# Weights and values in block order in DRAM, casts tied to TensorE, stores moved from ScalarE to SP

## The chip, the cores and the metric

The kernel runs on one core of a Trainium2 chip. A core has TensorE (PE; its weight loads are PEld), VectorE (DVE), ScalarE (ACT), GpSimd (POOL) and SyncE (SP), which only issues transfers, and 16 DMA engines that SP's and ScalarE's transfers share. The metric is device time in microseconds of one execution, as the median of several runs.

## The reference

Two layers of a hybrid backbone over 1024 latent and 256 context tokens of width 1024, in float32:

```
p = (layer_norm(x) * (1 + scale) + shift) @ w_in      # 7072 columns; ctx the same, with its own modulation
ya = neighbourhood attention(p[0:768])     # 4 heads of 64, 8x16 window, relative bias, plus the context
yb = latent attention(p[768:1184])         # low-rank q and kv, 4 heads, rotary key part
yc = bidirectional RG-LRU(p[1184:1440])    # conv of width 4, one linear scan per direction
yd = grouped-query attention(p[1440:1952]) # 4 heads, 2 kv heads, RMS norm, rotary
z, m = p[1952:2976], p[2976:7072]          # per branch: 256 columns of z, 1024 of m
out = sum_i sigmoid(m_i) * ((y_i * silu(z_i)) @ w_branch[i]) @ w_out
x = layer_norm(alpha * x + gate * out) * ln_g + ln_b
```

Every attention reads all context keys as well. Layer 1 needs the latent rows only.

## The kernel before, in words

All products are made of float32r pieces: each operand is split into a high part (a cast on ScalarE) and a low part (a subtraction on VectorE), and three matmuls replace one (`mm_a`, `mm_b`, lines 292 to 307). The modulated input stays in SBUF as `xh`, `xl`. Weights come through `load_w` (266): a DMA from SP into one of two `wraw` tiles, then `split_w` (248) casts (line 259) into `whi` and subtracts (260) into `wlo`. `load_chunk` (283) fetches a block of 1024 x 128 as two such loads of 512 rows, so a run in DRAM is 128 columns of a row of `w_in`, 512 B.

A layer runs through these stages, and the labels in front of tile names tell in which of them an instruction was written down:

- `g_proj`, `m_proj`, `a_proj` and `lru` project the tokens. `put_t` stores queries and keys transposed to DRAM, `put_v` (355) the values, token by token, by transfers from ScalarE.
- `g_att`, `m_att`, `a_att` are the attentions of branches D, B and A, four heads each. A head works through units of two or three query tiles of 128 (a unit of context queries first, in layer 0). `fetch` (907) loads the queries one unit ahead, `ahead_kv` (917) the next head's keys and values at a head's second unit (`i == 1`). The scores go to `wide` (line 660; 874 and 876 in branch A), VectorE takes the maximum (662), ScalarE the exponential (636, 640), TensorE transposes the probabilities (605), ScalarE and VectorE split them (310, 311) and TensorE multiplies them with the values (612, 613). The half sums are joined through a `tmp` tile (627). `load_q` (667) and `load_k` (678) read a source whose outermost dimension is two: 64 rows twice, or high and low part.
- Beside that, two fillings keep TensorE busy. `gates()` (941) computes 16 of the layer's 32 blocks of m (those in `gate_d`), in steps that `tick` hands out; each result is copied to a `tmp` tile (954) and stored from ScalarE (955). `put_u` (436), queued after every second head, computes a block of z, applies it to the head pair's output and stores that from ScalarE (466). It loads its weight block as it begins (438). `put_u` also ends each half of the LRU.
- `merge` loads the stored gates, or computes the other 16 blocks of m, multiplies with `w_branch` and sums; `outp` applies `w_out` and the layer norm.

There are three `tmp` tiles, two `wraw` tiles and, from the attention on, six pairs of `whi` and `wlo`, three blocks' worth.

The order in which an engine works is fixed before the run. The program is written down once, and a planner then puts each instruction onto its engine's queue as soon as, by its own estimate of durations, its inputs are there and a buffer is free; among those ready the one written down first goes first. An instruction can thereby move far ahead of its place in the program. On the chip each engine follows its queue in order and waits at semaphores.

Of the kernel before, what the change touches and what calls it, by code (L numbers as in the profile page):

```python
# [8 lines left out]
F32 = mybir.dt.float32  # L9
# [7 lines left out]
D = 1024  # L17
# [20 lines left out]
W_B = 26  # L38
UNITS = [(2, 3), (5, 3), (8, 2)]
# [7 lines left out]
def hybrid_kernel(ctx: ExitStack, tc, a):  # L47
# [200 lines left out]
    def split_w(raw, shape, far=False):  # L248

        n = 1  # L250
        for d in shape[1:]:
            n *= d
        if far:
            both = slot(F32R, w=1024, s="wboth")
            hi, lo = both[:, :512], both[:, 512:]
        else:
            hi = cut["wp"].tile([128, 512], F32R, tag="whi", name=nm("whi"))
            lo = cut["wp"].tile([128, 512], F32R, tag="wlo", name=nm("wlo"))
        act.copy(hi[:, :n], raw[:, :n])  # L259
# [6 lines left out]
    def load_w(src, shape, far=False):  # L266
# [8 lines left out]
        return split_w(raw, shape, far)  # L275
# [4 lines left out]
    def load_rows2(w2, c0):  # L280
        return [load_w(w2[k * 128:(k + 1) * 128, c0:c0 + 512], [128, 512]) for k in range(2)]

    def load_chunk(w2, c0, nk=KC):
        out = []
        for k0 in range(0, nk, 4):
            kk = min(4, nk - k0)
            hi, lo = load_w(w2[k0 * 128:(k0 + kk) * 128, c0:c0 + 128].rearrange("(k p) n -> p k n", p=128),
                            [128, kk, 128])
            out += [(hi[:, i, :], lo[:, i, :]) for i in range(kk)]
        return out  # L290
# [10 lines left out]
    def mm_b(ps, ws, xs, first=True, last=True):  # L301
        nk = len(ws)
        for k in range(nk):
# [3 lines left out]
            pe.matmul(ps, wl, xh, start=False, stop=last and k == nk - 1)  # L307
# [5 lines left out]
    def layer(l, xh, xl, need_ctx, gate, finish, side, ahead=None):  # L313
# [21 lines left out]
        v_a = dram([NT, 4, 128], F32, "va")  # L335
        v_m = dram([NT, 4, 128], F32, "vm")
        v_g = dram([NT, 2, 128], F32, "vg")
# [17 lines left out]
        def put_v(dst, t, src3):  # L355
# [4 lines left out]
            act.dma_start(dst[t * 128:(t + 1) * 128], vt.bitcast(F32)[:, :n, :])  # L360
# [75 lines left out]
        def put_u(i, c, y, rcp=None):  # L436

            w = load_chunk(w_in, C_Z + 256 * i + 128 * c)
# [27 lines left out]
            act.dma_start(u_d[i][c, :, QS], y[:, QS])  # L466
# [4 lines left out]
        def lru_steps():  # L471
# [24 lines left out]
            for c in range(2):  # L496
                wx = load_chunk(w_in, C_L + 128 * c)
# [65 lines left out]
                yield from put_u(2, c, hs[0])  # L563


        queue, later = [], []
# [85 lines left out]
        def dense_scores(ks, scale):  # L652
            def f(qs, qt, qi, total):
# [3 lines left out]
                for c0 in range(0, nk, 512):  # L657
                    w = min(512, nk - c0)
                    for j, k in enumerate(ks):
                        pe.matmul(wide[:, c0:c0 + w], qs[:, j, qi * 128:(qi + 1) * 128], k[:, c0:c0 + w],  # L660
# [24 lines left out]
        def load_v(d, h):  # L685
            t = kept("v", F32R, s="vs") if turn_kv[0] % 2 else slot(F32R, s="vs")
            t = t.rearrange("p (b e) -> p b e", e=128)
            sp.dma_start(t.bitcast(F32), d[:, h, :].rearrange("(b p) e -> p b e", p=128))
# [152 lines left out]
        def a_job(h):  # L841
# [7 lines left out]
            def begin(kv):  # L849
# [5 lines left out]
                def scores(qs, qt, qi, total):  # L855
# [19 lines left out]
                    for i in range(2):  # L875
                        pe.matmul(wide[:, 1024:1280], qsl[i], kd[:, :256], start=i == 0, stop=i == 1)
# [25 lines left out]
        def attention(jobs):  # L902
# [22 lines left out]
            for n, (job, i) in enumerate(steps):  # L925
# [4 lines left out]
                if i == 1:  # L930
                    j = jobs.index(job) + 1
                    if j < len(jobs):
                        ahead_kv(j)
                phase[0] = label
                scores, vt, (y, rcp) = head
                attend(h, units[i], qs.pop(n), y, rcp, scores, vt)
                if i == len(units) - 1 and h % 2:
                    queue.append([put_u(branch, h // 2, y, rcp), PUT])
                yield

        def gates():

            for i, c in gate_d:
                w = load_chunk(w_in, C_GATE + i * D + c * 128)
                for g in qgroups:
# [3 lines left out]
                    for k in range(0, KC, 2):  # L949
                        mm_b(ps[:, :g[1]], w[k:k + 2], lambda j: xs(k + j), k == 0, k == KC - 2)  # L950
# [4 lines left out]
                    act.dma_start(gate_d[i, c][:, gs], s[:, :g[1]])  # L955
# [301 lines left out]
```

## Time and profile before

| | us |
|---|---|
| median of 3 runs (lowest, highest) | 3084.11 (3082.05, 3084.87) |
| profiled execution | 3080.13 |
| its span, first to last instruction | 3078.3 |
| attention of layer 0, 430 to 1145 | 715 |
| attention of layer 1, 2041 to 2695 | 654 |

TensorE's mean granted clock is 0.96 of full speed. The DMA engines moved 301.82 MB. A stretch is named by its microseconds from the start of the span. A "wait" is idle time of an engine, put down to the instruction or transfer that ended last before it resumed; "issue" stands where the profile shows none.

### The profile page before, as it was taken

What the parts mean: (1) busy time and instruction counts of PE and PEld (TensorE: products, weight loads), DVE (VectorE), ACT (ScalarE), POOL (GpSimd) and SP (SyncE); (2) the same over time, 40 slices, a digit from 0 to 9 for tenths busy, and PEclk for the clock granted to TensorE, in tenths of its full rate; (3) what the DMA queues carried; (4) which work ended last, traced back from release to release, by engine and by line L of the source; (5) the groups of instructions that cost most, each with busy time, mean ns of one, the idle gap of its engine ahead of it and who ended that gap; (6) DMA issues with size and microseconds to landing.
All of it is one profiled execution on the core that took longest, in us unless ns stands there. A gap on an engine that the chain in (4) does not pass through costs nothing.

```text
span 3078.3 us, 40300 instructions
## 1 busy us (share of the span) xinstructions
PE 2815.5 (91%) x14458; PEld 2271.5 (74%) x14458; DVE 1549.3 (50%) x3151; ACT 1268.8 (41%) x2720; POOL 241.2 (8%) x363
## 2 busy tenths in 40 slices
PE   7988969998989899899998797989899798999998
PEld 3776848877878787667776686868778687777776
DVE  5653356654546452233458544257555465534456
ACT  4343255544445452222224335256445355532230
POOL 1210000000000000011122120000000000001121
PEclk9998989999999899999999898989999899999999
DMA  6333322222222324443432333322222233233332
GB/s 239 108 106 107 100 63 81 86 87 66 90 80 95 112 83 118 110 118 96 127 97 86 102 109 115 101 75 74 79 81 80 68 111 107 83 106 92 89 101 93
DMA packets 314912, 301.82 MB, mean 98 GB/s; under 512 B 24152, under 2 KB 253528, under 8 KB 314712
## 3 DMA queue, kind: packets, MB, share of 16 engines
q1 hardware_dynamic: 226776, 225.56, 24.5%
q10 hardware_dynamic: 87936, 73.68, 7.2%
q8 instruction: 114, 1.87, 0.3%
q14 instruction: 86, 0.70, 0.1%
HBM read 217.11 MB, written 82.07 MB: 97 GB/s over the span
## 4 chain that ended last, share of the span: by engine, by line
PE 71%; DMA 9%; DVE 6%; ACT 3%; issue 2%; SPq 2%; POOL 2%; ACTq 0%; DVEq 0%; POOLq 0%
PE wide L660 6%; PE merge__mm L305 4%; PE merge__mm L306 4%; PE merge__mm L307 4%; PE wide L305 3%; PE wide L306 3%; PE wide L307 3%; PE m_att__t L605 2%; PE a_att__mm L306 2%; PE a_att__mm L305 2%; PE a_att__mm L307 2%; PE g_att__t L605 2%; PE m_att__mm L307 2%; PE m_att__mm L306 2%; PE m_att__mm L305 2%
## 5 line engine op out<-in xcount | busy, mean ns | idle before, releaser
L305 PE MATMUL merge__mm<-xh,merge__whi 128*128 128x512 f32 (+1 forms) x640 | 243.2, 380 | 0.9 <-ACT a_att__tmp L954 0.9
L306 PE MATMUL merge__mm<-xl,merge__whi 128*128 128x512 f32 (+1 forms) x640 | 239.9, 375 | 0.0
L307 PE MATMUL merge__mm<-xh,merge__wlo 128*128 128x512 f32 (+1 forms) x640 | 239.6, 374 | 0.0
L311 DVE TENSOR_TENSOR m_att__pl<-m_att__t,m_att__ph 128x384 fp32r<-128x384 f32 (+1 forms) x248 | 121.8, 508 | 140.7 <-ACT m_att__ph L310 105.9
L259 ACT CAST merge__whi<-merge__wraw 128x256 fp32r<-128x256 f32 (+1 forms) x128 | 65.7, 513 | 255.4 <-PE merge__mm L306 176.9
L1022 DVE TENSOR_TENSOR merge__tmp<-wide,merge__tmp 128x512 f32<-128x512 f32 (+1 forms) x120 | 76.5, 637 | 182.4 <-PE wide L307 164.8
L305 PEld LDWEIGHTS merge__mm<-xh,merge__whi 128*128 128x128 f32 x640 | 120.7, 189 | 44.7 <-issue 19.5
L310 ACT CAST m_att__ph<-m_att__t 128x384 fp32r<-128x384 f32 (+1 forms) x248 | 104.8, 439 | 117.3 <-PE m_att__t L605 103.8
L311 DVE TENSOR_TENSOR g_att__pl<-g_att__t,g_att__ph 128x384 fp32r<-128x384 f32 (+1 forms) x228 | 111.2, 513 | 71.4 <-ACT g_att__ph L310 50.8
L260 DVE TENSOR_TENSOR merge__wlo<-merge__wraw,merge__whi 128x256 fp32r<-128x256 f32 (+1 forms) x128 | 72.8, 569 | 143.3 <-ACT merge__whi L259 135.2
L305 PE MATMUL wide<-merge__uh,merge__whi 128*128 128x256 f32 (+1 forms) x320 | 126.6, 396 | 18.3 <-ACT merge__uh L310 10.5
L307 PEld LDWEIGHTS merge__mm<-xh,merge__wlo 128*128 128x128 f32 x640 | 121.0, 189 | 24.2 <-issue 0.4
L306 PEld LDWEIGHTS merge__mm<-xl,merge__whi 128*128 128x128 f32 x640 | 120.9, 189 | 22.6
L660 PE MATMUL wide<-g_att__ks,g_att__q 128*128 128x512 f32 (+1 forms) x400 | 105.2, 368 | 26.6 <-DVE g_att__p L662 22.3
L305 PE MATMUL a_att__mm<-xh,a_att__whi 128*128 128x512 f32 (+1 forms) x320 | 124.8, 390 | 0.0
L1023 POOL TENSOR_TENSOR merge__acc<-merge__acc,merge__tmp 128x512 f32<-128x512 f32 (+1 forms) x60 | 78.1, 1302 | 586.1 <-DVE merge__tmp L1022 585.9
L310 ACT CAST g_att__ph<-g_att__t 128x384 fp32r<-128x384 f32 (+1 forms) x228 | 97.8, 446 | 60.8 <-PE g_att__t L605 55.9
L306 PE MATMUL a_att__mm<-xl,a_att__whi 128*128 128x512 f32 (+1 forms) x320 | 121.7, 380 | 0.0
L605 PE MATMUL m_att__t<-ident,m_att__p 128*128 128x128 f32 x616 | 107.8, 280 | 15.1 <-ACT m_att__p L636 7.6
L660 PE MATMUL wide<-m_att__ks,m_att__q 128*128 128x512 f32 (+1 forms) x400 | 117.8, 365 | 3.6 <-DVE m_att__p L662 3.6
L307 PE MATMUL a_att__mm<-xh,a_att__wlo 128*128 128x512 f32 (+1 forms) x320 | 121.0, 380 | 0.0
L306 PE MATMUL wide<-merge__ul,merge__whi 128*128 128x256 f32 (+1 forms) x320 | 119.0, 372 | 0.1
(418 smaller groups left out, 7867.5 us busy)
## 6 DMA issues: line engine op xcount, KB each, us to landing
merge__wraw<-in_w_in_dram SPq DMA_DIRECT2D x64, 256.0 KB
mod__wm<-in_w_mod_dram SPq DMA_DIRECT2D x64, 256.0 KB
g_proj__wm<-in_w_mod_dram SPq DMA_DIRECT2D x16, 512.0 KB
a_att__wraw<-in_w_in_dram SPq DMA_DIRECT2D x32, 256.0 KB
merge__wraw<-in_w_branch_dram SPq DMA_DIRECT2D x64, 128.0 KB
merge__tmp<-start__gates SPq DMA_DIRECT2D x32, 256.0 KB
merge__tmp<-outp__gates SPq DMA_DIRECT2D x32, 256.0 KB
g_att__wraw<-in_w_in_dram SPq DMA_DIRECT2D x28, 256.0 KB
```

The lines of the kernel that those rows point to most:

```text
L259: act.copy(hi[:, :n], raw[:, :n])
L260: dve.tensor_sub(lo[:, :n], raw[:, :n], hi[:, :n])
L305: pe.matmul(ps, wh, xh, start=first and k == 0, stop=False)
L306: pe.matmul(ps, wh, xl, start=False, stop=False)
L307: pe.matmul(ps, wl, xh, start=False, stop=last and k == nk - 1)
L310: act.copy(hi, src)
L311: dve.tensor_sub(lo, src, hi)
L605: pe.transpose(tb[:, i * 128:(i + 1) * 128], pts[q0 + i][:, col:col + 128], ident)
L660: pe.matmul(wide[:, c0:c0 + w], qs[:, j, qi * 128:(qi + 1) * 128], k[:, c0:c0 + w], start=j == 0, stop=j == len(ks) - 1)
L1022: dve.tensor_mul(sgm[:, :g[1]], pb[:, :g[1]], sgm[:, :g[1]])
L1023: (pool if w is None else dve).tensor_add(acc[c][:, gs], acc[c][:, gs], sgm[:, :g[1]])
```

## The change

`w_in` is divided on the host: its first 1952 columns stay as they were, and the blocks of 128 columns that `load_chunk` reads (2 of the LRU, 8 of z, 32 of m) become `w_chunks`, in which a partition's eight rows of 128 columns lie one behind the other; a load of half a block reads 2 KB runs. `w_branch` is arranged likewise (1 KB). The values in DRAM change from token-major to head-major: `put_v` writes runs of 512 B, where it wrote one run per token, and `load_v` reads one run of 5 KB per partition, where it read ten of 512 B.

`split_w` takes an instruction `after` and makes the cast wait for it. The blocks of z in the attention are loaded at the second unit of a head pair's second head and their casts wait for the last score matmul written down until then. A gate block's casts wait for the last matmul of the first quarter of the previous block's second column group; the first block of a layer has none. The gate stores, and the u stores of the attentions, go from ScalarE to SP; those of the LRU stay.

```diff
+LATER = mybir.DependencyInfo(mybir.DependencyClass.Sync, mybir.DependencyReason.DATA)
+Z_0, GATE_0 = 2, 10
...
-    def split_w(raw, shape, far=False):
+    def split_w(raw, shape, far=False, after=None):
...
-        act.copy(hi[:, :n], raw[:, :n])
+        cast = act.copy(hi[:, :n], raw[:, :n])
+        if after is not None:
+            tc.add_manual_dep(cast.ins, after.ins.name, LATER, reason="the load has until then")
...
-    def load_chunk(w2, c0, nk=KC):
+    def load_chunk(w3, after=None):
+
         out = []
+        nk = w3.shape[1]
         for k0 in range(0, nk, 4):
             kk = min(4, nk - k0)
-            hi, lo = load_w(w2[k0 * 128:(k0 + kk) * 128, c0:c0 + 128].rearrange("(k p) n -> p k n", p=128),
-                            [128, kk, 128])
+            hi, lo = load_w(w3[:, k0:k0 + kk, :], [128, kk, 128], after=after)
...
-        v_a = dram([NT, 4, 128], F32, "va")
-        v_m = dram([NT, 4, 128], F32, "vm")
-        v_g = dram([NT, 2, 128], F32, "vg")
+        v_a = dram([4, 128, TT, 128], F32, "va")
+        v_m = dram([4, 128, TT, 128], F32, "vm")
+        v_g = dram([2, 128, TT, 128], F32, "vg")
...
-            act.dma_start(dst[t * 128:(t + 1) * 128], vt.bitcast(F32)[:, :n, :])
+            act.dma_start(dst[:, :, t, :].rearrange("h p e -> p h e"), vt.bitcast(F32)[:, :n, :])
...
-        def put_u(i, c, y, rcp=None):
-
-            w = load_chunk(w_in, C_Z + 256 * i + 128 * c)
+        def load_z(i, c, after=None):
+            return load_chunk(a["w_chunks"][l, Z_0 + 2 * i + c], after)
+
+        def put_u(i, c, y, w, rcp=None):
+
...
-            act.dma_start(u_d[i][c, :, QS], y[:, QS])
+            (act if rcp is None else sp).dma_start(u_d[i][c, :, QS], y[:, QS])
...
-                yield from put_u(2, c, hs[0])
+                yield from put_u(2, c, hs[0], load_z(2, c))
...
-                        pe.matmul(wide[:, c0:c0 + w], qs[:, j, qi * 128:(qi + 1) * 128], k[:, c0:c0 + w],
+                        newest[0] = pe.matmul(wide[:, c0:c0 + w], qs[:, j, qi * 128:(qi + 1) * 128], k[:, c0:c0 + w],
...
-            sp.dma_start(t.bitcast(F32), d[:, h, :].rearrange("(b p) e -> p b e", p=128))
+            sp.dma_start(t.bitcast(F32), d[h])
...
                     if j < len(jobs):
                         ahead_kv(j)
+                    if h % 2:
+                        wz = load_z(branch, h // 2, newest[0])
...
-                    queue.append([put_u(branch, h // 2, y, rcp), PUT])
+                    queue.append([put_u(branch, h // 2, y, wz, rcp), PUT])
...
+            half = None
             for i, c in gate_d:
-                w = load_chunk(w_in, C_GATE + i * D + c * 128)
+                w = load_chunk(a["w_chunks"][l, GATE_0 + i * KC + c], half)
...
-                        mm_b(ps[:, :g[1]], w[k:k + 2], lambda j: xs(k + j), k == 0, k == KC - 2)
+                        last = mm_b(ps[:, :g[1]], w[k:k + 2], lambda j: xs(k + j), k == 0, k == KC - 2)
+                        if k == 0 and g == qgroups[1]:
+                            half = last
...
-                    act.dma_start(gate_d[i, c][:, gs], s[:, :g[1]])
+                    sp.dma_start(gate_d[i, c][:, gs], s[:, :g[1]])
...
-                    w = None if (i, c) in gate_d else load_chunk(w_in, C_GATE + i * D + c * 128)
-                    wb = load_chunk(a["w_branch"][l, i], c * 128, 2)
+                    w = None if (i, c) in gate_d else load_chunk(a["w_chunks"][l, GATE_0 + i * KC + c])
+                    wb = load_chunk(a["w_branch"][l, i, c])
```

## Rows read from the trace of the kernel before

**Rows 1.** The page, part 1: busy us (share of the span) xinstructions.
```profile
PE 2815.5 (91%) x14458; PEld 2271.5 (74%) x14458; DVE 1549.3 (50%) x3151; ACT 1268.8 (41%) x2720; POOL 241.2 (8%) x363
```

**Rows 2.** Windows: stretch, us, busy PE PEld DVE ACT POOL, clock, DMA share, GB/s.
```profile
430.00:1145.00 715.00, 669.87 (x3873) 569.07 (x3874) 393.57 (x894) 360.75 (x812) 11.81 (x34) 0.96 0.27 86
1145.00:1550.00 405.00, 392.91 (x1939) 292.99 (x1938) 140.44 (x238) 107.48 (x221) 49.55 (x45) 0.99 0.40 115
...
2041.00:2695.00 654.00, 591.84 (x3253) 493.24 (x3254) 370.31 (x786) 333.14 (x719) 9.59 (x28) 0.95 0.28 86
2695.00:2955.00 260.00, 257.46 (x1081) 200.28 (x1080) 98.89 (x159) 76.36 (x140) 29.15 (x21) 1.00 0.33 95
```

**Rows 3.** Waits of PE, attention of layer 0: us in total, times, longest us.
```profile
PE wide L660 <- DVE g_att__p L662: 22.1, 2, 21.5
PE a_att__pv L612 <- ACT a_att__ph L310: 13.2, 2, 9.4
PE m_att__pv L612 <- ACT m_att__ph L310: 9.8, 1, 9.8
PE m_att__t L605 <- ACT m_att__p L636: 7.6, 1, 7.6
PE wide L660 <- DVE m_att__p L662: 3.6, 1, 3.6
```

**Rows 4.** Waits of PE, attention of layer 1.
```profile
PE m_att__pv L612 <- ACT m_att__ph L310: 16.8, 1, 16.8
PE g_att__mm L305 <- issue: 12.7, 1, 12.7
PE a_att__t L605 <- DVE a_att__pl L311: 11.8, 2, 11.6
PE g_att__pv L612 <- ACT g_att__ph L310: 8.3, 1, 8.3
PE m_att__t L605 <- DVE m_att__pl L311: 7.3, 1, 7.3
PE wide L660 <- DMA g_att__q<-outp__qkg: 2.2, 1, 2.2
```

**Rows 5.** Timeline, layer 0: start us, us, what [idle before <-releaser].
```profile
732.52 3.68 SPq L674 DMA_DIRECT2D m_att__q<-start__qkm  x1
...
736.09 0.33 ACTq L955 DMA_DIRECT2D start__gates<-m_att__tmp  x1
...
736.46 0.65 ACT L310 CAST m_att__ph<-m_att__t 128x256 fp32r<-128x256 f32 x2 [10.68 <-DMA m_att__q<-start__qkm]
...
887.67 1.36 ACT L636 ACTIVATE m_att__p<-m_att__p,m_att__nb 128x1280 f32<-128x1280 f32 x1 [8.34 <-DMA m_att__q<-start__qkm]
...
1007.42 0.62 ACT L259 CAST a_att__whi<-a_att__wraw 128x512 fp32r<-128x512 f32 x1 [4.92 <-DMA a_att__q<-start__qka]
```

**Rows 6.** Tile a_att__whi: count, ns min/median/max, first and last start us.
```profile
L305 PE MATMUL a_att__mm<-xh,a_att__whi x320: 277/394/776, 922.8 to 2691.8; 128*128 128x512 f32 x128, 128*128 128x256 f32 x32
...
L259 ACT CAST a_att__whi<-a_att__wraw x32: 603/620/627, 824.8 to 2628.4; 128x512 fp32r<-128x512 f32 x32
```

**Rows 7.** Timeline, layer 1, around 2400 us: SP's issues and ScalarE's cast.
```profile
2393.95 13.46 SPq L674 DMA_DIRECT2D m_att__q<-outp__qkm  x1
...
2411.54 3.24 SPq L274 DMA_DIRECT2D a_att__wraw<-in_w_in_dram  x2
...
2421.39 0.62 ACT L259 CAST a_att__whi<-a_att__wraw 128x512 fp32r<-128x512 f32 x1 [17.73 <-DMA a_att__wraw<-in_w_in_dram]
```

**Rows 8.** Windows of single stretches, columns as in rows 2.
```profile
2.00:18.00 16.00, 9.35 (x32) 0.78 (x32) 4.57 (x9) 0.22 (x1) 1.82 (x4) 1.00 1.00 378
848.00:858.00 10.00, 9.96 (x59) 8.39 (x57) 5.61 (x11) 5.42 (x12) 0.00 (x0) 1.00 0.13 52
2422.00:2426.00 4.00, 3.56 (x9) 2.78 (x10) 1.62 (x3) 2.12 (x5) 0.00 (x0) 0.50 0.51 168
```

**Rows 9.** The chain that ended last, layer 0: start us, us, what.
```profile
984.15 22.83 DMA a_att__q<-start__qka
```

More of the change, by code (lines that the diff above doesn't have):

```diff
@@ L264, in split_w, with load_w @@
         return hi[:, :n], lo[:, :n]
-    def load_w(src, shape, far=False):
+    def load_w(src, shape, far=False, after=None):
         n = 1
@@ L274, in load_w @@
         sp.dma_start(dst, src)
-        return split_w(raw, shape, far)
+        return split_w(raw, shape, far, after)
     def load_rows(w2, c0, n):
         return [load_w(w2[k * 128:(k + 1) * 128, c0:c0 + n], [128, n]) for k in range(KC)]
-    def load_rows2(w2, c0):
-        return [load_w(w2[k * 128:(k + 1) * 128, c0:c0 + 512], [128, 512]) for k in range(2)]
-    def load_chunk(w2, c0, nk=KC):
+    def load_chunk(w3, after=None):
         out = []
+        nk = w3.shape[1]
         for k0 in range(0, nk, 4):
             kk = min(4, nk - k0)
-            hi, lo = load_w(w2[k0 * 128:(k0 + kk) * 128, c0:c0 + 128].rearrange("(k p) n -> p k n", p=128),
-                            [128, kk, 128])
+            hi, lo = load_w(w3[:, k0:k0 + kk, :], [128, kk, 128], after=after)
             out += [(hi[:, i, :], lo[:, i, :]) for i in range(kk)]
@@ L306, in mm_b @@
             pe.matmul(ps, wh, xl, start=False, stop=False)
-            pe.matmul(ps, wl, xh, start=False, stop=last and k == nk - 1)
+            end = pe.matmul(ps, wl, xh, start=False, stop=last and k == nk - 1)
+        return end
     def hi_lo(hi, lo, src):
@@ L496, in lru_steps @@
             for c in range(2):
-                wx = load_chunk(w_in, C_L + 128 * c)
+                wx = load_chunk(a["w_chunks"][l, c])
                 x = slot(s="lrux")
@@ L562, in lru_steps @@
                 dve.tensor_add(hs[0][:, QS], hs[0][:, QS], hs[1][:, QS])
-                yield from put_u(2, c, hs[0])
-        queue, later = [], []
+                yield from put_u(2, c, hs[0], load_z(2, c))
+        queue, later, newest = [], [], [None]
         def step():
@@ L875, in scores @@
                     for i in range(2):
-                        pe.matmul(wide[:, 1024:1280], qsl[i], kd[:, :256], start=i == 0, stop=i == 1)
+                        newest[0] = pe.matmul(wide[:, 1024:1280], qsl[i], kd[:, :256], start=i == 0, stop=i == 1)
                     dve.tensor_tensor_reduce(pt[:, :n], wide[:, w0:w0 + n], bias[:, bo:bo + n], 1.0, NEG,
@@ L1234 @@
         "cc": np.stack([f(c)[0], f(c_ctx)], -1).reshape(8, 128, 2).transpose(1, 0, 2),
-        "w_mod": f(w_mod), "b_mod": cols(b_mod, 24), "w_in": f(w_in),
+        "w_mod": f(w_mod), "b_mod": cols(b_mod, 24), "w_in": f(w_in)[:, :, :C_Z],
+        "w_chunks": np.concatenate([f(w_in)[:, :, C_L:C_G], f(w_in)[:, :, C_Z:]], 2)
+        .reshape(L, KC, 128, 42, 128).transpose(0, 3, 2, 1, 4),
         "na_bias": rel[:, :, bidx],
@@ L1242 @@
         "gqa_q_norm": f(gqa_q_norm), "gqa_k_norm": f(gqa_k_norm),
-        "w_branch": f(w_branch), "w_out": f(w_out), "ln_g": f(ln_g), "ln_b": f(ln_b),
+        "w_branch": f(w_branch).reshape(L, 4, 2, 128, KC, 128).transpose(0, 1, 4, 3, 2, 5), "w_out": f(w_out), "ln_g": f(ln_g), "ln_b": f(ln_b),
         "rope_c": rope_c, "rope_s": rope_s, "mrope_c": mrope_c, "mrope_s": mrope_s,
```

## The prediction

> **What bounds the kernel now.** Four views, in this order. The page's first part: TensorE is busy for 2815.5 us, 91% of the span [rows 1], every other engine for half or less. TensorE is the bound, so only its idle time and its slow clock can be won. The same by stretch [rows 2]: in the two merges it works 392.9 of 405 us and 257.5 of 260, so a transfer that lands earlier there buys at most 12 + 2.5 us. In the two attentions it works 669.9 of 715 us and 591.8 of 654: 45 + 62 = 107 us idle, the DMA engines being 27 to 28% busy.
>
> Third, what ended that idle time [rows 3, 4]. The reader is to see few, long waits:
> - layer 0: 22.1 (two, the long one 21.5 at the seam with the LRU), 13.2 (two: 9.4 and 3.8), 9.8, 7.6 and 3.6 us;
> - layer 1: 16.8, 12.7, 11.6 of 11.8, 8.3, 7.3 and 2.2 us.
>
> Nearly all name ScalarE or VectorE as releaser, although these are busy for only half of the stretch. Fourth, therefore, ScalarE's own timeline ahead of each, which shows two different obstacles.
>
> *A transfer that ScalarE issues.* At 736.09 it issues a gate store (L955, 0.33 us), and the cast behind it has waited 10.68 us [rows 5]. SP was at that time held for 3.68 us on a single issue of its own. The same stands ahead of 887.67 (8.34 us) and 1007.42 (4.92 us). TensorE's part: 9.8 + 7.6 + 3.8 = 21.2 us [rows 3].
>
> *A cast whose weight has not landed.* At 2421.39 the cast at L259 has waited 17.73 us for its DMA [rows 7]. It is a tile named for the third attention, cast in the second: the planner puts a cast onto ScalarE's queue as soon as it believes the load done and a buffer free. The first such cast in the trace stands at 824.8, the first matmul that reads one at 922.8 [rows 6]: 98 us early. Nobody needs the cast, but ScalarE works in order, and the softmax stands behind it. The load was late because SP issued it only at 2411.54, after 13.46 us on one query transfer [rows 7]. Six waits of this kind, from the timelines ahead of each: 3.6 and 9.4 in layer 0, 16.8, 11.6, 8.3 and 7.3 in layer 1: 57.0 us [rows 3, 4].
>
> **The change part by part.** The sum is made against the profiled execution (3080.1 us outside, span 3078.3); the median of the runs is 3084.1, 4 us above, so I add the difference to that.
>
> *1. Stores leave ScalarE.* 16 gate blocks per layer with 3 and 2 column groups make 80 gate stores, and with 12 u stores 92 issues of 0.33 us go to SP: 30 us of ScalarE, which is not the bound, so 0 directly. What counts is the three blocked ones: -21.2 us. Ends: 0 (all three stall anew elsewhere) and -21.2; I take the latter, because no other issue of ScalarE is left in the attention that could block it.
>
> The Trainium skill says otherwise (page "DMA: Bandwidth & Descriptors", section "Issuing engines are not separate DMA queues"): choosing the issuing engine saves only the sequencer's issue time, usually small. By it this part would be worth nothing, and the forecast 21 us later. The 10.68 us in front of a 0.33 us issue speak against it.
>
> *2. Casts are tied to TensorE.* 30 of the 32 gate blocks (the first of a layer has no predecessor) and 12 z blocks get a wait. A gate block's cast now comes no sooner than the first quarter of the previous block's second group, step 5 of 12 or of 8, while its load can start when the raw buffers are free, about one block sooner: 715/16 = 45 us for a load that took about 10 (2411.54 to 2421.39). Behind the waiting cast stand softmax and the casts of probabilities; the wait is for a matmul that is already in TensorE's queue, so it costs ScalarE time but TensorE none as long as it has matmuls ahead. What can stay: z and gates share two raw buffers, so a gate load behind a late z can only start when its due point has passed, and is then cast with the planner's short margin. Each z displaces one gate block, in about half of the cases past its due point: 6 of 42 blocks with the old margin, and I double that for the new plan's own misjudgements. Against 6 long waits in 44 blocks, that leaves 1 or 2 of 9.5 us: 14 us. Taken: 57 - 14 = -43. Ends: -57 and 0.
>
> *3. Clock.* After such a wait TensorE restarts slowly: the granted clock over 2422 to 2426 is 0.50, the lower of its two levels, with 3.56 us of work in it [rows 8]. Half of that, some 1.7 us, is lost per wait. Nine waits are addressed (three and six), 7.5 of them go: -13. Ends: -15 and 0.
>
> *4. Long runs.* The 42 blocks, the 16 blocks per layer that the merge still loads and LRU weights come in 2 KB runs instead of 512 B, w_branch in 1 KB, and the 20 value loads in 5 KB. At the start the load of long-run weights moves 378 GB/s at a DMA share of 1.00 [rows 8]; the attention moves 86 at 0.27, or 319 at a full share [rows 2]. So at best a sixth of these transfers' own time goes, and of a 10 us landing most is waiting. For TensorE: 0, ends -5 and 0. In the merges: 0, ends -14 and +3. The price: 60 value stores in the projections now write four (two) 512 B runs per row instead of one of 2 KB (1 KB). ScalarE still issues them; the transposed keys next to them already go out in 512 B runs. 0, ends -3 and +5.
>
> *5. What SP gets.* 92 more issues in order, each waiting for ScalarE's copy, with the query, key and weight loads queued behind. SP's 0.33 us each (30 us of 1369) are hidden while the query loads run one unit ahead; so far TensorE waited for a query only once, 2.2 us [rows 4]. Below: 0. Above: the second rival. Near the 2.2 us row, a handful of such waits plus some held buffers: +15.
>
> *6. What does not move.* The long runs do not change the two-row loads. Query and key loads have an outermost source dimension of two (a broadcast, or the high and low halves), and while only they run, the DMA share is 0.13, two of 16 engines, at 52 GB/s [rows 8]; a 640 KB key takes 12.6 us there. With TensorE faster, they come due sooner: +5, ends 0 and +40 (first rival). The seam at the LRU (21.5) and the first gate block of layer 1 (12.7, untied) stay; ends for these two -34 and +10, as the new plan may shift them.
>
> The Trainium skill has this rule (same page, "Rules for kernel authors"): an outermost dimension below 16 confines a DMA to as many engines. The trace agrees (0.13), and it is the reason to distrust part 4.
>
> Sum: -21 - 43 - 13 + 15 + 5 = -57. Layer 0's attention goes from 715 to about 690, layer 1's from 654 to about 621. 3084 - 57 = **3027 us**.
>
> **The rivals.**
>
> *First: the two engines of the query and key loads become the bound.* Per head of the second attention in layer 0 these are 1.31 MB of query, 0.66 of rotary query and 0.66 of key: 2.62 MB at 52 GB/s, 50 us, of 715/12 = 60 us per head. All else is 0.27 - 0.13 x 50/60 = 0.16 of each engine, another 10 us: there is no room. Then the waits of the second attentions (9.8, 7.6, 3.6, 16.8, 7.3: 45 us, of which the sum counts some 38) come back as waits for queries, less the 5 already charged: about 3060. For it: SP's 13.46 us on one query issue [rows 7]. Against it: TensorE's only visible wait for a query is 2.2 us, and the first and third attentions have no rotary query. This is where the skill's rule in part 6 leads.
>
> *Second, the other side: the gate stores hold buffers.* A gate's copy sits in one of three `tmp` tiles until its store has landed; the values' halves and the z products use the same three. The attentions use 80 + 84 + 30 = 194 of them in 1369 us, one each 7.1 us, so a tile is wanted again after 21 us. On ScalarE's queue nothing waited for them. On SP's, the store stands behind query loads, of which one took 22.83 us from issue to landing [rows 9], after SP's own delay. If half of the 80 stores come 5 us too late for the next user, ScalarE stalls, as now, for 200 us, of which TensorE's queue covers perhaps half: +100 instead of +15, hence 3084 - 77 + 5 + 100 = 3112. It decides from (77 - 5) / 80 = 0.9 us per store. Against it: the 21 us are long compared with most landings.
>
> *Third: the change fully does what it says*: -21 - 57 - 15, and 0 to SP: 2991.
>
> *Fourth: the planner's new order is as wrong as the old*: the tie is a lower bound only, and stalls of the old size reappear at z casts and query loads. 3078 to 3090.
>
> **How the numbers follow.** Forecast, 3000 to 3050: 0.50. First rival, 3050 to 3078: 0.13. Third, below 3000: 0.15. Fourth: 0.08. Second: 0.14. A measurement of this kernel tells 0.2%, 6 us, from no change. Faster 0.78, within 0.2% 0.08, slower 0.14. The range runs from 2980 (the third plus half of the seam's stalls) to 3088, which leaves out most of the second rival and a little below. The forecast's own range is 3000 to 3050.
>
> **What would show it.** Part 1: no DMA issue on ScalarE's queue in the attentions, and no ScalarE idle time of 5 to 11 us ahead of a probability cast with no late weight. Part 2: no cast that waits for its DMA by more than 6 us, but for the first block of a layer, and the first cast of a third-attention weight within some 45 us of its first matmul instead of 98. Part 3: granted clock 0.97 or more there. Part 5: SP's waits at the gate stores, and TensorE's waits for a query below 15 us. First rival: DMA share still 0.13 in long pieces, waits for query or key. Second rival: ScalarE's copies waiting for gate transfers. Wrong altogether: the attentions stay at 715 and 654, or the time moves in projections or merges by over 10 us.

## The result, and the profile after

The changed kernel takes 3119.67 us (four runs, 3118.14 to 3121.57) against 3083.08 for the kernel before on the same chip: 1.0123 of it, 95% interval 1.0105 to 1.0140. It is 37 us slower where 56 us less was forecast.

The page's first part, busy time, share and instructions, against [rows 1]: TensorE's work is the same and the span longer.

```profile
PE 2819.3 (90%) x14458; PEld 2274.4 (73%) x14458; DVE 1545.8 (50%) x3151; ACT 1262.2 (40%) x2720; POOL 242.0 (8%) x363
```

The windows by stage, columns as in [rows 2]: attention of layer 0, merge, attention of layer 1, merge.

```profile
430.00:1177.00 747.00, 670.85 (x3871) 568.86 (x3872) 393.52 (x895) 359.62 (x813) 12.08 (x34) 0.95 0.24 82
1177.00:1582.00 405.00, 392.33 (x1935) 292.92 (x1934) 136.75 (x235) 105.06 (x217) 50.19 (x44) 0.99 0.38 115
2074.00:2734.00 660.00, 593.55 (x3252) 494.79 (x3253) 369.67 (x785) 330.31 (x720) 9.58 (x28) 0.95 0.25 86
2734.00:2994.00 260.00, 258.34 (x1086) 201.37 (x1085) 99.32 (x162) 76.22 (x143) 30.03 (x22) 1.00 0.30 95
```

The merges are as long as before. The attentions have grown by 32 and 6 us, with TensorE's busy time within 2 us of [rows 2]: the loss is idle time in the two attentions. TensorE's waits there (us in total, times, longest), layer 0 against [rows 3]:

```profile
PE a_att__pv L617 <- ACT a_att__ph L313: 23.2, 2, 19.1
PE wide L665 <- DVE g_att__p L667: 20.2, 3, 19.4
PE g_att__pv L617 <- ACT g_att__ph L313: 15.8, 2, 15.5
PE m_att__pv L618 <- DVE m_att__pl L314: 15.5, 1, 15.5
PE m_att__pv L617 <- DVE g_att__y L634: 8.0, 1, 8.0
PE m_att__t L610 <- ACT m_att__p L641: 3.3, 1, 3.3
```

and layer 1 against [rows 4]:

```profile
PE g_att__mm L307 <- ACT g_att__whi L261: 18.1, 1, 18.1
PE a_att__pv L618 <- DVE a_att__pl L314: 13.7, 1, 13.7
PE g_att__mm L307 <- issue: 12.6, 1, 12.6
PE m_att__pv L617 <- ACT m_att__ph L313: 12.0, 2, 6.2
PE g_att__t L610 <- DVE g_att__pl L314: 5.8, 1, 5.8
```

The seam (20.2) and the first gate block (12.6) are about as before (22.1 and 12.7). The rest sorts by what ScalarE was held up by just before. ScalarE's timeline (start, us, line, operation, in brackets its idle time before it and what ended that):

```profile
473.75 1.14 ACT L261 CAST g_att__whi<-g_att__wraw 128x512 fp32r<-128x512 f32 x2 [0.32 <-PE wide L665]
...
499.39 1.26 ACT L261 CAST g_att__whi<-g_att__wraw 128x512 fp32r<-128x512 f32 x2 [16.99 <-DMA g_att__wraw<-in_w_chunks_dram]
...
752.41 0.37 ACT L632 COPY m_att__tmp<-m_att__pv 64x256 f32<-64x256 f32 x1 [10.62 <-DMA start__gates<-m_att__tmp]
...
899.66 0.62 ACT L261 CAST m_att__whi<-m_att__wraw 128x512 fp32r<-128x512 f32 x1 [16.05 <-DMA m_att__wraw<-in_w_chunks_dram]
...
1005.40 0.62 ACT L261 CAST a_att__whi<-a_att__wraw 128x512 fp32r<-128x512 f32 x1 [0.57 <-PE wide L665]
...
1031.67 0.62 ACT L261 CAST a_att__whi<-a_att__wraw 128x512 fp32r<-128x512 f32 x1 [20.41 <-DMA a_att__wraw<-in_w_chunks_dram]
```

Nine casts wait over 5 us (5.6 to 20.4) for a weight that has not landed, besides the first block of layer 1. TensorE's part is 23.2 + 15.8 + 15.5 in layer 0 and 18.1 + 13.7 + 12.0 + 5.8 in layer 1: 104 us, where six such casts cost 57 before. No issue blocks ScalarE any more (21.2 before), but two copies wait for a gate store to leave their `tmp` tile (8.0 + 3.3). Together 115.4 us (104.1 + 11.3) against 78.2 (57.0 + 21.2), +37 us: as much as the whole loss.

Why these weights are late stands on SP (DMA issues: start, us that SP was held, line):

```profile
479.29 14.26 SPq L278 DMA_DIRECT2D g_att__wraw<-in_w_chunks_dram  x2
...
886.04 3.84 SPq L850 DMA_DIRECT2D a_att__be<-in_na_bias_dram  x1
889.94 0.42 SPq L851 DMA_DIRECT2D a_att__bm<-in_na_bias_dram  x1
890.46 0.85 SPq L278 DMA_DIRECT2D m_att__wraw<-in_w_chunks_dram  x2
...
1006.76 4.69 SPq L850 DMA_DIRECT2D a_att__be<-in_na_bias_dram  x1
1011.54 8.55 SPq L851 DMA_DIRECT2D a_att__bm<-in_na_bias_dram  x1
1020.14 0.51 SPq L677 DMA_DIRECT2D a_att__q<-start__qka  x1
1020.74 4.15 SPq L278 DMA_DIRECT2D a_att__wraw<-in_w_chunks_dram  x2
```

ScalarE reached the cast that ran at 1031.67 at 1011.26 (1031.67 - 20.41). SP issued its load only at 1020.74, 9.5 us after that, having been held for 13.24 us on two bias loads (4.69 + 8.55); the weight then took another 11 us to land. Ahead of 899.66 the load came 6.9 us after ScalarE had got there. Ahead of 499.39 it came 3.1 us before, with SP held for 14.26 us on its two issues.

### The profile page after: what moved, and what is told of

It reads as the page before. It is cut to its first block, busy times and chain, and to the rows that moved or that the text cites. A ratio compares the mean times of both kernels' runs of the same rounds, so it can differ in the third digit from the quotient of the medians.

```text
span 3116.7 us, 40317 instructions
## 1 busy us (share of the span) xinstructions
PE 2819.3 (90%) x14458; PEld 2274.4 (73%) x14458; DVE 1545.8 (50%) x3151; ACT 1262.2 (40%) x2720; POOL 242.0 (8%) x363
## 4 chain that ended last, share of the span: by engine, by line
PE 70%; DMA 8%; DVE 6%; ACT 3%; issue 2%; SPq 2%; POOL 2%; ACTq 0%; DVEq 0%; POOLq 0%
PE wide L665 5%; PE merge__mm L307 4%; PE merge__mm L308 4%; PE merge__mm L309 4%; PE wide L307 3%; PE wide L308 3%; PE wide L309 3%; PE m_att__t L610 2%; PE g_att__t L610 2%; PE a_att__mm L307 2%; PE a_att__mm L308 2%; PE a_att__mm L309 2%; PE m_att__mm L309 2%; PE m_att__mm L308 2%; PE m_att__mm L307 2%
## 5 line engine op out<-in xcount | busy, mean ns | idle before, releaser
L308 PE MATMUL merge__mm<-xl,merge__whi 128*128 128x512 f32 (+1 forms) x640 | 240.2, 375 | 0.0
L307 PE MATMUL wide<-merge__uh,merge__whi 128*128 128x256 f32 (+1 forms) x320 | 126.6, 396 | 18.1 <-ACT merge__uh L313 9.8
L308 PEld LDWEIGHTS merge__mm<-xl,merge__whi 128*128 128x128 f32 x640 | 121.2, 189 | 22.8
L307 PE MATMUL g_att__mm<-xh,g_att__whi 128*128 128x512 f32 (+1 forms) x256 | 101.6, 397 | 32.1 <-ACT g_att__whi L261 18.1
L665 PE MATMUL wide<-g_att__ks,g_att__q 128*128 128x512 f32 (+1 forms) x400 | 104.3, 368 | 22.8 <-DVE g_att__p L667 20.7
L314 DVE TENSOR_TENSOR a_att__pl<-a_att__t,a_att__ph 128x384 fp32r<-128x384 f32 (+2 forms) x204 | 91.6, 462 | 59.5 <-ACT a_att__ph L313 37.5
L308 PE MATMUL wide<-merge__ul,merge__whi 128*128 128x256 f32 (+1 forms) x320 | 119.4, 373 | 0.0
L309 PE MATMUL wide<-merge__uh,merge__wlo 128*128 128x256 f32 (+1 forms) x320 | 119.1, 372 | 0.0
L667 DVE TENSOR_SCALAR_CACHE_REDUCE m_att__p<-wide 128x1280 f32<-128x1280 f32 (+1 forms) x72 | 98.6, 1370 | 41.1 <-PE wide L665 40.9
L665 PE MATMUL wide<-m_att__ks,m_att__q 128*128 128x512 f32 (+1 forms) x400 | 118.4, 369 | 0.1
```

What stands on the lines that cost most here:

```text
L307: pe.matmul(ps, wh, xh, start=first and k == 0, stop=False)
L308: pe.matmul(ps, wh, xl, start=False, stop=False)
L309: end = pe.matmul(ps, wl, xh, start=False, stop=last and k == nk - 1)
L314: dve.tensor_sub(lo, src, hi)
L665: newest[0] = pe.matmul(wide[:, c0:c0 + w], qs[:, j, qi * 128:(qi + 1) * 128], k[:, c0:c0 + w], start=j == 0, stop=j == len(ks) - 1)
L667: dve.tensor_scalar(pt[:, :nk], wide[:, :nk], -scale, None, ALU.mult, ALU.min, accum_out=nb)
```

## The experiments

Theories, as they stood when the first four ran. A: a tied cast of z keeps both raw tiles, so the gate block behind it is loaded late. B: loads land late because the two-row query and key loads fill two DMA engines, whatever the buffers do. C: the stores on SP are what costs. All ratios are to the kernel before on the same chip. "Raw tile" is a `wraw` tile, a "tie" the wait that the change adds to a cast, and a load's "landing" the time from its issue to its end.

| | kernel | us | ratio, 95% interval |
|---|---|---|---|
| e1 | changed, z weights in a raw tile of their own | 3119.96 | 1.0109 [1.0089, 1.0130] |
| e2 | changed, z untied and loaded at its use | 3123.07 | 1.0126 [1.0101, 1.0151] |
| e3 | e2 and gates untied | 3092.48 | 1.0016 [1.0005, 1.0027] |
| e4 | changed, stores back on ScalarE | 3131.04 | 1.0148 [1.0128, 1.0168] |
| e5 | changed, queries and keys on 64 rows | 2960.71 | 0.9611 [0.9595, 0.9627] |
| e6 | before, queries and keys on 64 rows | 2964.47 | 0.9623 [0.9608, 0.9637] |
| e7 | changed, gate ties one group earlier | 3158.92 | 1.0252 [1.0232, 1.0272] |
| e8 | changed, gates untied, z tied | 3159.29 | 1.0256 [1.0240, 1.0271] |
| e9 | long runs only | 3078.30 | 0.9988 [0.9979, 0.9997] |
| e10 | changed, two-row loads cut in two by columns | 3154.37 | 1.0238 [1.0224, 1.0252] |
| e11 | e5 without any tie | 2964.22 | 0.9619 [0.9606, 0.9632] |
| e12 | changed, only queries on 64 rows | 3014.25 | 0.9780 [0.9767, 0.9793] |
| e13 | e1, z loaded one unit earlier | 3031.85 | 0.9827 [0.9811, 0.9843] |
| e14 | changed, no waits, z load where the change has it | 3088.74 | 1.0018 [1.0008, 1.0028] |
| e15 | e13 without any tie | 3106.26 | 1.0088 [1.0073, 1.0103] |
| e16 | e13, queries and keys on 64 rows | 2958.94 | 0.9608 [0.9592, 0.9624] |

**Which part costs: e1 to e4, e8, e9.** The edit of e1:

```diff
+            raw, out = slot(w=1024, s="zraw"), []
+            for h in range(2):
+                hs = slice(512 * h, 512 * h + 512)
+                sp.dma_start(raw[:, hs].rearrange("p (a b) -> p a b", a=4), w3[:, 4 * h:4 * h + 4, :])
+                hi, lo = split_w(raw[:, hs], [128, 4, 128], after=after)
```

> The changed kernel, with the raw weights of the tied z blocks in a tile of their own (one of the 14 slots) in place of the two shared raw tiles. Theory A (a tied z cast keeps both raw tiles, so the next gate block is loaded late and its cast, whose due point is past, stalls ScalarE): the waits of 15.5, 15.5, 19.1, 18.1, 13.7 and the three of about 6 us nearly all go, 3120 becomes 3030 to 3045. Theory B (loads land late because the query and key loads fill two DMA engines, whatever the buffers): waits of the same number return elsewhere, 3100 to 3120. Theory C (stores on SP cost the time): 3110 to 3120.

No gain, so theory A alone does not explain the loss. In e1 the gate casts no longer wait for a load, but for the first block of layer 1. Now the z casts do, at the same places. ScalarE, and then SP's issue of that weight:

```profile
1036.55 0.62 ACT L261 CAST a_att__whi<-a_att__zraw 128x512 fp32r<-128x512 f32 x1 [19.81 <-DMA a_att__zraw<-in_w_chunks_dram]
```

```profile
1027.72 0.86 SPq L446 DMA_DIRECT2D a_att__zraw<-in_w_chunks_dram  x2
```

The tile was another, yet the load stood as late in SP's queue as the other had, behind the same two bias loads and 8.8 us ahead of its cast's start. Over the twelve z blocks of e1, SP issues the load between 9 us before ScalarE gets to the cast and 11 us after that (median 2.8 before).

In e2 `put_u` loads z as it begins, as before the change, and in e3 the gates lose their tie too:

```diff
-                    if h % 2:
-                        wz = load_z(branch, h // 2, newest[0])
...
+            w = load_z(i, c)
```

> The changed kernel, with the z blocks loaded untied where put_u begins, as before; gate blocks stay tied, stores stay on SP, long runs stay. Theory A: no z keeps raw tiles any more, but a z that comes while a tied gate block holds them is itself late: 3040 to 3080. Theory B: 3100 to 3120. Theory C: 3110 to 3120.

```diff
-                w = load_chunk(a["w_chunks"][l, GATE_0 + i * KC + c], half)
+                w = load_chunk(a["w_chunks"][l, GATE_0 + i * KC + c])
```

> The changed kernel without any tie (z loaded where put_u begins, gates untied): long runs and stores on SP alone. Theory A: the ties are what costs, so this is before less ScalarE's three blocked stores plus the tmp waits of 11 us: 3065 to 3085. Theory B: about as before, 3075 to 3095. Theory C: still 3105 to 3120.

```diff
-            (act if rcp is None else sp).dma_start(u_d[i][c, :, QS], y[:, QS])
+            act.dma_start(u_d[i][c, :, QS], y[:, QS])
...
-                    sp.dma_start(gate_d[i, c][:, gs], s[:, :g[1]])
+                    act.dma_start(gate_d[i, c][:, gs], s[:, :g[1]])
```

> The changed kernel with its gate and u stores issued by ScalarE again; ties and long runs stay. Theories A and B: the tmp waits of 8.0 and 3.3 us go, and some 20 us of blocked issues come back: 3120 to 3135. Theory C: most of the loss goes, 3080 to 3095.

Taking off the z ties alone changes nothing, taking off all ties gives back about 28 us (3120 to 3092), and going back to ScalarE for the stores does not help. So the loss is in the ties; C fell. e8 takes off the gate ties alone (same edit as e3):

> The changed kernel with gate casts untied; z casts stay tied. e2 (gates tied, z not) was as slow as both ties, e3 (no ties) within 0.2% of the kernel before. If the cost of the gate ties alone is the loss: 3090 to 3100. If either tie by itself costs the whole 28 us, because one late cast in the two raw tiles is enough: 3110 to 3125.

It is slower than both ties together, by 39 us and beyond what either case had said, so either tie alone costs, and they do not add up. e9 is e3 with the edit of e4, which leaves the layout alone:

> The changed kernel without its ties and with its stores back on ScalarE: only the layout in long runs is left. The forecast gave it 0 (ends -17 and +8); the run without ties, which has the stores on SP as well, came out 0.2% above the kernel before. 3075 to 3095 if the layout is worth nothing; under 3070 would mean that shorter landings of weights count.

The layout is worth 0.9 to 6.5 us. e9 and e3 differ only by the stores on SP: 0.9988 to 1.0016, some 9 us lost. What became of the three blocked issues of [rows 5] is seen on ScalarE in e3, at the first and the last of their places:

```profile
746.60 0.37 ACT L633 COPY m_att__tmp<-m_att__pv 64x256 f32<-64x256 f32 x1 [9.49 <-DMA start__gates<-m_att__tmp]
...
1004.41 0.58 ACT L963 COPY a_att__tmp<-a_att__mm 128x512 f32<-128x512 f32 x1 [12.22 <-DMA start__gates<-a_att__tmp]
```

The issue no longer blocks ScalarE; the copy that wants the same `tmp` tile does (10.68 and 4.92 us before). At the second place it is 3.91 us where it was 8.34.

**Is it the time at which the raw tile comes free: e7.**

```diff
-                        if k == 0 and g == qgroups[1]:
+                        if k == 0 and g == qgroups[0]:
```

> The changed kernel with the tie of each gate block moved one column group earlier, to the first quarter of the first group of the block before (in layer 0 about a third of a block, some 15 us, in layer 1 half a block, some 20 us). Theory A' (a tied cast gives its raw tile back late, so that the next load is issued with only the planner's few us ahead of its cast): raw tiles come free 15 to 20 us sooner and the stalls shrink to those of the run without ties: 3090 to 3105. Theory B (the engines, not the tie, make landings late): no change, 3112 to 3125.

Slower by another 39 us, against both expectations. Earlier release does not help, and the load gains no lead over its own cast: ahead of the cast at 504.72 SP issued it at 484.7, 3 us before ScalarE got there, as in the changed kernel. There is also a new cast wait of 18.61 us at 764.89. e8, which has no gate ties at all, stalls at the same places (16.88 us at 502.37, 19.13 at 762.90) and takes as long: the earlier gate tie is worth no more than none, and what both keep are the z ties on the shared raw tiles.

**Are the two-row loads the root: e5, e6, e10 to e12.** The edit of e5 and e6, and the same for the rotary part and the keys; bytes and their order in SBUF stay:

```diff
-                sp.dma_start(tf[:, i, :nq], d[i, blk, r0:r0 + 64, t0:t0 + nq][None].to_broadcast([2, 64, nq]))
+                for j in range(2):
+                    sp.dma_start(tf[64 * j:64 * j + 64, i, :nq], d[i, blk, r0:r0 + 64, t0:t0 + nq])
```

> The changed kernel with the query and key loads split in two, so that each has 64 (32 for the rotary part) rows outermost instead of 2; bytes and runs stay, SP issues up to twice as many. Theory B (a block's load lands 6 to 20 us after its issue because query and key loads fill two DMA engines, and its few pieces on those two land last): landings come down to some 5 us, all long waits of casts go, TensorE gains 70 to 100 us of the 104 us of cast waits: 3020 to 3060. Theory A' (the ties release raw tiles late, the load is issued late, whatever the engines do): landings hardly change, 3100 to 3120. More issues on SP alone would give 3125 to 3140.

> The kernel before with the same split of query and key loads and nothing else. Theory B: its casts that waited for a landing (57 us of TensorE's waits) and its stores blocked behind loads (21 us) lose most of their cause: 3020 to 3050. Theory A': landings hardly change, 3080 to 3095.

Both gain more than theory B had said, 117 to 120 us against before. Windows of e5 in layer 0's attention (columns as in [rows 2]), then its DMA issues of the second attentions of both layers (KB each, median us to landing):

```profile
430.00:1090.00 660.00, 655.44 (x3858) 556.20 (x3859) 386.22 (x865) 358.09 (x809) 12.09 (x34) 1.00 0.30 91
```

```profile
m_att__wraw<-in_w_chunks_dram SPq DMA_DIRECT2D x28, 256.0 KB, 3.0
m_att__q<-start__qkm SPq DMA_DIRECT2D x32, 96.0 KB, 2.5
m_att__ks<-start__qkm SPq DMA_DIRECT2D x8, 320.0 KB, 4.7
```

TensorE works 655 of 660 us at full clock. A weight lands 3.0 us after its issue, where the two above had taken 9 and 11 us.

Why it lands late in the changed kernel is in its trace too, which has the times at which a load raised its semaphore, sixteen times for a weight. Ahead of the cast at 1031.67, fourteen of them lie between 1026.15 and 1026.93 and the last two at 1030.77 and 1031.65. Over the 88 weight loads of the two attentions, fourteen have come after 3.05 us and all after 7.05 (medians), and in 56 loads the last two are over 2 us behind. In e5 the medians are 2.82 and 3.04, and no load has its last two that far behind. So it is two parts of sixteen that are late, as many as the engines that the two-row loads keep busy (0.13 of 16 [rows 8]). In the kernel before the medians are 3.37 and 7.07: the change did not make landings longer, it left less time for them.

No cast, copy or issue of ScalarE waits 5 us for a transfer in the two attentions. With both kernels so close, the 37 us of the change are gone too: the ties cost only while landings are long. e10 is the control, with as many and as large DMAs as e5, each still on two rows (and with runs half as long as e5's, which it does not separate):

```diff
+                m = nq // 2
+                for j in (0, m):
+                    sp.dma_start(tf[:, i, j:j + m],
+                                 d[i, blk, r0:r0 + 64, t0 + j:t0 + j + m][None].to_broadcast([2, 64, m]))
```

> Control for the split of e5: the changed kernel with each query and key load cut in two by columns, so that SP issues as many and as large DMAs as in e5, but each still has two rows outermost. Theory B (two engines carry all of it): no gain, 3100 to 3150, DMA share still 0.13 or less while only they run. If instead smaller pieces, more of them, or the plan that follows from them made e5 fast: 2960 to 3020.

```profile
430.00:1090.00 660.00, 576.73 (x3331) 488.21 (x3332) 342.15 (x731) 309.80 (x676) 8.81 (x22) 0.94 0.24 80
```

Slower than the change, with TensorE idle for 83 of 660 us. A weight's last two parts are still over 2 us behind in 35 of 88 loads. So neither more pieces nor smaller ones, nor the plan that follows from their number, made e5 fast; the rows did. e11 is e3 with the edit of e5, and e12 that edit at the queries alone:

> e5 without any tie (long runs, stores on SP, query and key loads split to 64 rows): with landings of some 3 us, what are the ties worth? By the theory that a tie costs only because a late issue meets a long landing, they cost nothing here: 2955 to 2968, as e5 (2960.7) and e6 (2964.5). If holding the raw tiles costs by itself, it is 2925 to 2945; if early casts still cost TensorE, 2975 or more.

> The changed kernel with only the query loads split to 64 rows; the 20 key loads stay on two rows. Per head of the second attention, queries are 1.97 of 2.62 MB of two-row bytes. If the stream of queries is what keeps the two engines full: most of the gain of e5, 2965 to 3000. If the 320 or 640 KB of one key, 6 to 13 us at 52 GB/s, are enough to make the weights behind it late: 3030 to 3090.

e11 can't be told from e5 or e6: with short landings, ties are worth nothing either way. e12 lies between its two forecasts, 67 us under before, a little over half of e5's 120: the stream of queries is the larger part, and the 20 key loads still cost some 54 us (3014.25 - 2960.71).

**Why ties meet more long landings: e13 to e16.** e13 keeps e1's tile and the tied cast where it was, and moves the load from a head's second unit to its first, ahead of the next head's keys and values (`z_raw` is the load of e1, `z_cast` its casts):

```diff
                 if i == 0:
                     head = begin(kv[label, h])
+                    if h % 2:
+                        zr = z_raw(branch, h // 2)
...
-                        wz = load_z(branch, h // 2, newest[0])
+                        wz = z_cast(zr, newest[0])
```

> The changed kernel with the raw z weights in a tile of their own (as e1) and their load issued one attention unit earlier, at a head's first unit, ahead of the next head's key and value loads instead of behind them; the tied cast stays where it was. If what the ties lack is distance between issue and cast (the load sits behind the two-row key, query and bias loads, 8 to 19 us before its cast): the z stalls of e1 go (its six longest are 12 to 20 us each on ScalarE), 3040 to 3070. If another load then stands in the same place and stalls in its stead: 3090 to 3125.

> The changed kernel with every wait for TensorE taken off its casts, but with the z loads still called where the change calls them, at a head's second unit right behind the next head's key and value loads (the run without ties had moved them back to the end of the head as well). If the waits themselves cost the 28 us: as the run without ties, 3085 to 3097. If the place of the z load costs it: 3110 to 3130.

e13 is 1.7% faster than before: 3031.85 us, below the 3040 to 3070 expected of it, with 88 us less than e1 for one moved load. That it lies 5 us from the forecast is luck: part 1's 21 us did not come here either (two copies of layer 0 wait 13.09 and 7.45 us for gate stores). Landings are as long as in the changed kernel (median 7.15 us), so it is the lead that pays: SP issues a z load 5 to 18 us before ScalarE gets to its cast (median 12.8, where e1 had 2.8). Its waits and windows in layer 1:

```profile
PE g_att__mm L307 <- issue: 12.5, 1, 12.5
PE wide L894 <- DVE a_att__pa L899: 8.0, 2, 7.4
PE merge__mm L307 <- ACT a_att__tmp L981: 0.9, 1, 0.9
```

```profile
2090.00:2570.00 480.00, 478.00 (x2697) 400.16 (x2696) 296.74 (x616) 266.99 (x578) 7.80 (x22) 1.00 0.28 95
```

No cast of the two attentions waits 5 us for a load but that of the first block. e14, with the place kept and only the waits taken off, falls back to the kernel before: the place of the z load costs nothing by itself. How the casts lie without ties, on ScalarE and then SP in e14:

```profile
506.70 0.62 ACT L261 CAST g_att__whi<-g_att__wraw 128x512 fp32r<-128x512 f32 x1 [0.68 <-PE g_att__mm L308]
...
512.26 0.62 ACT L261 CAST g_att__whi<-g_att__wraw 128x512 fp32r<-128x512 f32 x1 [0.45 <-PE g_att__mm L308]
...
541.31 0.62 ACT L261 CAST g_att__whi<-g_att__wraw 128x512 fp32r<-128x512 f32 x1 [0.56 <-PE g_att__mm L308]
```

```profile
508.53 0.34 SPq L278 DMA_DIRECT2D g_att__wraw<-in_w_chunks_dram  x1
...
515.18 2.14 SPq L278 DMA_DIRECT2D g_att__wraw<-in_w_chunks_dram  x1
```

These untied casts come one half-block at a time, as matmuls of a gate (L308) give back a `whi` and `wlo`, so they were already paced by TensorE. A raw tile is filled again 2 to 3 us after its cast and, of two tiles in turn, read by the cast after the next: the load of 508.53 has until 541.31, 33 us. In the changed kernel both halves of a block go at once (473.75, 1005.40 and 1006.19). Both raw tiles come free together, and the next block gets only the time until its own tied cast: 482.4 - 474.9 = 7.5 us in the first of these cases, 1011.3 - 1006.8 = 4.5 us in the other. In both the first block is one of z, tied to a score matmul (`PE wide L665` in the lines above), and the second one of a gate. Where gate follows gate the time is long: a load issued at 538.50 has until 586.34, 48 us.

One thing was left open by this: whether the ties earn e13's gain, or the tile and early load alone.

> e13 (z weights in a tile of their own, loaded one unit earlier) with every wait for TensorE taken off the casts. e13 came out at 0.9827 of the kernel before, 58 us under the kernel without ties. If the ties earn that, as the forecast's part 2 has it: back to 3070 to 3095 here. If the tile of its own and the early load earn it by themselves: 3020 to 3045.

> e13 together with the query and key loads on 64 rows. If nothing of the casts' waits is left to win once landings are 3 us: 2955 to 2968, as e5. Under 2950 would mean that the two gains add up.

e15 is 2.6% slower than e13 (1.0088 to 0.9827), and above the 3070 to 3095 expected: the ties earn about 80 us once the load is early. Without them ScalarE gets to a z cast 3 to 4 us after the load's issue, for all twelve. Untied, z casts run ahead and wait for their load, on ScalarE in e15:

```profile
737.71 0.62 ACT L261 CAST m_att__whi<-m_att__zraw 128x512 fp32r<-128x512 f32 x1 [11.92 <-DMA m_att__zraw<-in_w_chunks_dram]
...
879.61 1.29 ACT L261 CAST m_att__whi<-m_att__zraw 128x512 fp32r<-128x512 f32 x2 [11.83 <-DMA m_att__zraw<-in_w_chunks_dram]
...
2344.51 0.62 ACT L261 CAST m_att__whi<-m_att__zraw 128x512 fp32r<-128x512 f32 x1 [15.70 <-DMA m_att__zraw<-in_w_chunks_dram]
...
2475.67 0.62 ACT L261 CAST m_att__whi<-m_att__zraw 128x512 fp32r<-128x512 f32 x1 [16.75 <-DMA m_att__zraw<-in_w_chunks_dram]
```

e16 equals e5: the gains of early loads and of spread loads are the same microseconds. e5, e6, e11 and e16 beat both kernels, and can't be told apart; the smallest edit of them is e6.

## Why the prediction was wrong

**The step that failed is the one in part 2 that gave a tied block's load "about one block sooner: 715/16 = 45 us" and left 14 us of cast waits.** That time is there where a gate block follows a gate block. Two raw tiles hold just one block, a tied block frees them as a pair, and z and gate ties come at unrelated times, so a block whose tie fell soon after another's had little: over the nine stalls 1.4 to 14 us lie between the end of the casts before and ScalarE's arrival (7.5 and 4.5 in the two cases above), and the weight came 5.6 to 20.4 us after ScalarE had got there. The text saw that ("z and gates share two raw buffers") and counted such blocks about rightly, "6 of 42 blocks with the old margin", doubled to twelve. What it had wrong is how often they stall: as rarely as blocks did before, 6 in 44, which left one or two waits of 9.5 us. But there were nine, at nine of the twelve places where a z block comes in, of 11.6 us each on average: 104 us instead of 14. With a tile of its own (e1) the z load still had too little time, because SP reached it late; tile and place in SP's queue together (e13) gave it.

The tie itself worked as described. The tile `a_att__whi` in the changed kernel, as in [rows 6]:

```profile
L307 PE MATMUL a_att__mm<-xh,a_att__whi x280: 275/394/736, 946.0 to 2731.1; 128*128 128x512 f32 x112, 128*128 128x256 f32 x28
...
L261 ACT CAST a_att__whi<-a_att__wraw x28: 603/620/635, 916.1 to 2694.6; 128x512 fp32r<-128x512 f32 x28
```

The first cast of a third-attention weight comes 30 us ahead of its first matmul instead of 98. With the distance supplied (e13), the tie does what part 2 says, and e15 shows that it is the tie that does it.

*Part 1, -21.2.* No issue of ScalarE is left that blocks it, as forecast; the time did not come. The stall passed to the copies that want the same tile (e3: 9.49 and 12.22 us; the changed kernel: 11.3 us of TensorE's time). Parts 1 and 5 together, -21 + 15 in the sum, measured some +9 without ties (e9 to e3). With ties the stores on SP look better by 8 us (e4 to the changed kernel), but those two intervals overlap. The Trainium skill's rule that the prediction set aside (page "DMA: Bandwidth & Descriptors", section "Issuing engines are not separate DMA queues": the choice of issuing engine saves only issue time) described this better than the forecast. What held the 0.33 us issue up were the transfers in front of it, and these stayed.

*Part 3, -13.* The granted clock is 0.95 in both attentions against 0.96 and 0.95: the long waits did not go, so neither did the lower clock behind them. It was 1.00 in the stretches of e5 and e13 without waits, so the step followed part 2's fate.

*Part 4, 0.* Right: -0.9 to -6.5 us alone (e9), the merges unchanged.

*Part 6 and the first rival.* The two engines were the root of the long landings in the attentions: a late weight waits for its last two parts of sixteen, with the two-row loads spread both kernels fall to about 2960 (e5, e6), and cutting them without spreading does not help (e10). The rival named the resource and looked for the wrong victim. It priced waits for queries (3060) and was set back because TensorE waited for a query for only 2.2 us [rows 4]. The queries, issued a unit ahead, were in time; the weights and gate stores queued behind them paid.

*The other rivals.* The second, on the slower side, names a wait that did appear (`tmp` tiles held by stores), but at 11.3 us of its 100, and without it (e4) the time is no better. The fourth had the right wait, a stall of the old size at casts, and took for granted that there would be no more of them than before. The seam and the first gate block stayed, as said.

Not shown: why e7 and e8 lose 39 us more than the change. Their traces have the same waits and some more (764.89 in e7, 762.90 in e8), and no run was made to tell which of SP's neighbours causes these. More raw tiles for the gate blocks, the early z load without a tile of its own, and a longer landing in the planner's own estimates were not tried.

## What to carry to other kernels

Ask of a late transfer first what lies in front of it, on its issuing queue and on its engines: here one outermost dimension of two, in loads that TensorE waited for by only 2.2 us, cost 117 us. A wait that holds a consumer back helped here only with the load issued early and into a buffer that was free, so give the load its distance before tying its cast, and count buffers in blocks, not tiles. A stall that ends on a transfer moved to the next user of the same buffer when only the issuing engine was changed.

## What the runs showed of the hardware

- SP was held by an issue while two-row transfers stood in front: two weight issues took 14.26 us, one query issue 11.99, in the changed kernel. With 64 rows outermost (e5) 671 of SP's 690 issues in the attentions (430 to 1090 and 1997 to 2570 us) took under 0.65 us, the longest 1.6.
- The same 256 KB weight lands after 3.0 us beside loads of 64 rows, and after 7.05 beside loads of two rows (medians of e5 and the changed kernel; 9 and 11 at the two casts above). Its own runs, 512 B or 2 KB, hardly matter: 2.9 and 3.0 us in the second attention of e6 and e5. The Trainium skill (page "DMA: Bandwidth & Descriptors", section "Rules for kernel authors") has the cause, an outermost dimension below 16 confining a DMA to as many engines; the DMA share of 0.13 agrees [rows 8]. That it delays the weights issued behind it is what these runs show: their last two parts of sixteen come over 2 us late in 56 of 88 loads, in none of e5.
